# Two GpSimd subtractions of a transformer layer, each cut into pieces of 256 columns

## The chip, the cores and the metric

The kernel runs on one core of a Trainium2 chip. A core has a matrix engine (TensorE, PE in the profile, with its weight loads as PEld), VectorE (DVE), ScalarE (ACT), GpSimd (POOL) and SyncE (SP, which here only issues DMA transfers). Each engine works off its own queue of instructions in order; semaphores make one wait for another. The metric is the time of one execution on the device in microseconds, and a kernel's time is the median of several runs. The profile is one further execution, recorded by the hardware profiler.

## The reference

The function is one layer of a diffusion backbone: 128 context tokens (the prompt) and 512 sample tokens, 640 in all, of width 1024. Cut to what matters here:

```python
def project(h, w_in):                       # 1024 -> 2304 columns
    z = h @ w_in
    qa, ka, va, qb, kb, vb = jnp.split(z, ...)   # 8 neighbourhood heads, 8 window heads on 2 key groups
# for the prompt and for the sample tokens:
h = modulate(rmsnorm(x, g_mix_pre), sh1, sc1)
qa, ka, va, qb, kb, vb = project(h, w_in)        # sample: qb, kb also get a rotary embedding
oa = neighborhood_attn(qa, ka, va, cache_a_k, cache_a_v, rpb_a)
ob = window_attn(qb, kb, vb, cache_b_k, cache_b_v, sink_b)
x = x + gt1 * rmsnorm(concat(rmsnorm(oa, g_a), rmsnorm(ob, g_b)) @ w_out, g_mix_post)
h = modulate(rmsnorm(x, g_ffn_pre), sh2, sc2)
x = x + gt2 * rmsnorm(conv_ffn(h, w_up, conv_w, conv_b, w_down), g_ffn_post)
```

All inputs are fp32, and `sh`, `sc`, `gt` come from a product of the conditioning vectors with `w_mod` (1024 x 6144).

## The kernel before, in words

**Two parts for every operand.** The matrix products run on fp32r operands. Every factor is therefore kept as a high part (`act(hi, src)`, a copy on ScalarE into fp32r) and a low part (`lo = src - hi`), and each product is three matmuls: high by high, high by low, low by high (`mm3`). The low part is a subtraction of two tensors in SBUF, `tt(lo, src, f(hi), ALU.subtract)`, and runs on VectorE, or on GpSimd where `eng=nc.gpsimd` is given. All such subtractions show under line 111 of the profile (the helper `tt`), all ScalarE copies under 108 (`act`), all matmuls of products under 127 (`mm`).

**The stages.** Up to about 60 us the tokens are normalised, transposed and modulated, and the values of the neighbourhood heads are computed. From there to about 330 us the projections and the attention run interleaved. About 280 to 380 us hold the output projection and the second norm, then comes the expansion of the feed-forward part with its convolution (tiles `zx`, `yy`, `wsum`, `ou`, `osb`, to about 650 us), then the contraction (`psd`).

**The streamed weight blocks.** The columns of `w_in` for queries and keys (and the values of the window heads) come in 14 blocks of 1024 x 128, one tile `[128, 8, 128]` each: 1024 columns per partition. The class `Stream` handles them: `load` issues the DMA (line 338, tile `wst`, on SyncE's queue), `split` makes `wh` on ScalarE and `wl` by a subtraction and then issues the next load, and `take` hands a pair to a projection. The pairs have two buffers. The low part of block 0 is made half on VectorE and half on GpSimd, of blocks 1 and 2 on VectorE, of blocks 3 to 13 whole on GpSimd. A projection `tgemm` runs in two chunks of 320 tokens and calls `split` in the middle of the second one; the two projections of one head pair, the keys and values of the window heads and their four query blocks follow each other this way. `tgemm` also carries small products for the modulation (`side_gen`: tiles `wms`, loaded at line 821, results copied to `T` by ScalarE before the next matmuls).

**The attention.** It is a hand-written pipeline of jobs, one per 128 query tokens and head pair. `Pipe.slot` emits the steps of three jobs in turn, and `fill_run` emits steps of the projections between them by estimated costs; so the order on every engine is fixed when the program is built. In a job, TensorE makes the scores (`psS`), VectorE adds the bias or mask and takes the maximum (line 626), ScalarE exponentiates (`P`), the softmax is scaled by VectorE for one head (`soft2`, line 116, tile `P`) and by ScalarE for the other, TensorE transposes (`psT`), and the high and low parts (`ptH`/`ptL`, `pwH`/`pwL`) are made by ScalarE and VectorE. The window heads' queries and keys pass through `rope` on VectorE (tiles `rx`, with a shuffle at line 933) before they are split into `qb` or `kvU`.

**The heads' outputs.** When a head pair's four jobs are done, `o_put` splits its output `o` (512 sample tokens, or 128 prompt tokens) into `oa` or `ob`: the high part on ScalarE, the low part on GpSimd. For the neighbourhood heads the columns are permuted on the way (`jview`, `jsrc`). GpSimd then also adds up squares (`wmsk`, `cs`), clears corners of `ptH`/`ptL`, and copies parts of the bias table (`tab`).

Of the kernel before, what the change touches and what calls it, by code (L numbers as in the profile page):

```python
# [11 lines left out]
ALU = mybir.AluOpType  # L12
# [3 lines left out]
KD = 8  # L16
# [10 lines left out]
def trunk_kernel(  # L27
# [8 lines left out]
    nc = tc.nc  # L36
# [47 lines left out]
    def PB(shape, name, dt=F32):  # L84
        return pp_.tile(shape, dt, tag="p", name=name)
# [15 lines left out]
    def PS(kind, name):  # L101
        return PSB[kind].tile([128, 512], F32, tag=kind, name=name)

    def f(ap):
        return ap.bitcast(F32)

    def act(out, in_, func=ACTF.Copy, **kw):
        return nc.scalar.activation(out=out, in_=in_, func=func, **kw)  # L108

    def tt(out, a, b, op, eng=None):  # L110
        return (eng or nc.vector).tensor_tensor(out=out, in0=a, in1=b, op=op)  # L111
# [10 lines left out]
    def split(hi, lo, src):  # L122
        act(hi, src)
        tt(lo, src, f(hi), ALU.subtract)
# [203 lines left out]
    class Stream:  # L328
# [13 lines left out]
        def split(self):  # L342
            if self.ns < len(self.srcs):
                wh = wr_.tile([128, KD, 128], F32R, tag="wh", name="wh")
                wl = wr_.tile([128, KD, 128], F32R, tag="wl", name="wl")
                w = self.w.pop(self.ns)
                act(wh, w)
                if self.ns:
                    tt(wl, w, f(wh), ALU.subtract, eng=nc.vector if self.ns < 3 else nc.gpsimd)
                else:  # L350
                    for s_, e in ((slice(0, 4), nc.vector), (slice(4, 8), nc.gpsimd)):
                        tt(wl[:, s_], w[:, s_], f(wh[:, s_]), ALU.subtract, eng=e)
                self.s[self.ns] = (wh, wl)
                self.ns += 1
                if self.ns > 1:
                    self.load()
# [163 lines left out]
    def wtile(src, f0):  # L520
        w = WS([128, KD, 128], "wst")
        nc.sync.dma_start(out=w, in_=src[:, f0:f0 + 128].rearrange("(k p) f -> p k f", p=128))
        wh = wr_.tile([128, KD, 128], F32R, tag="wh", name="wh")
        wl = wr_.tile([128, KD, 128], F32R, tag="wl", name="wl")
        split(wh, wl, w)
        return wh, wl
# [42 lines left out]
    def k_ctx(kt, src, step, cnt):  # L569
        def dst(i):  # L570
            v = kt[:, i, :]
            return bass.AP(tensor=v.tensor, offset=v.offset, ap=[list(v.ap[0]), [step, cnt], [1, 128]])
        split(dst(0), dst(1), src.unsqueeze(1).to_broadcast([128, cnt, 128]))
# [10 lines left out]
    def qk_gen(p):  # L584
# [4 lines left out]
        w = stream.take()  # L589
        ps0 = yield from tgemm(w, 0)  # L590
        pend.append(lambda: split(q[:, 0, 0:320], q[:, 1, 0:320], ps0[:, 0:320]))
        ps1 = yield from tgemm(w, 1)
        pend.append(lambda: split(q[:, 0, 320:640], q[:, 1, 320:640], ps1[:, 0:320]))
# [65 lines left out]
    def o_put(o, N, dH, dL, view, t0, n, ss, then=None):  # L659


        act(dH, view(o[:, 0:N]))
        tt(dL, view(o[:, 0:N]), f(dH), ALU.subtract, eng=nc.gpsimd)
        nt = N // 128
        acc = sq_acc["a" if ss is ssA else "b"]
        ac = acc[:, t0 * 128:t0 * 128 + N]
        sqt = PB([128, 512], "sqt")[:, 0:N] if n else ac
        act(jview(sqt) if view is jsrc else sqt, view(o[:, 0:N]), ACTF.Square)
        if n in (1, 2):
            tt(ac, ac, sqt, ALU.add, eng=nc.gpsimd)  # L670
        if n < 2 or (n == 2 and t0):
            return
        if n == 2:
            sqt, t0, nt = acc, 0, 5
        yield 0.22 * nt
        ps_ = PS("o", "psst")
        for t in range(nt):
            nc.tensor.matmul(ps_[:, 2 * t:2 * t + 2], sqt[:, t * 128:t * 128 + 128], ones, start=True, stop=True)
        yield 0.0
        tt(ss[:, t0:t0 + nt], ss[:, t0:t0 + nt], ps_[:, 0:2 * nt:2], ALU.add)  # L680
        if then and n == 2:
            then()
# [5 lines left out]
    jsrc = lambda t: t.rearrange("p (j r c) -> p j r c", j=8, r=8)  # L688

    def natten_jobs(p):  # L690
# [35 lines left out]
        def fin():  # L726
            vc = QK[p][2]
            o = PB([128, 512], "o32")
            for e in range(2):
                ob = PS("o", "psO")  # L730
                h = 2 * p + e
                V = lambda t: Vt[h // 4][:, t, h % 4, :, :].rearrange("p s d -> p (s d)")
                B = lambda a, b, n: tuple(x[:, a:b:n, :] for x in pts[e])
                pv_mm(ob, [
                    (slice(0, 512), vc[:, e, :, :].rearrange("p s d -> p (s d)"), *B(2, 12, 3)),
                    (slice(0, 256), V(2), *B(1, 4, 2)),
                    (slice(128, 384), V(3), *B(4, 7, 2)),
                    (slice(256, 512), V(4), *B(7, 10, 2)),
                    (None, V(1), *B(0, 11, 10)),
                ])  # L740
                yield 0.0 if e else 1.5
                o_sum(o, ob, e, 512)
            yield 0.0
            yield from o_put(o, 512, jview(oa[0][:, p, 128:640]), jview(oa[1][:, p, 128:640]), jsrc, 1, p, ssA)
# [4 lines left out]
    def prompt_job(qkt, ko, V, dst, n, ss, sk, then=None):  # L749
# [43 lines left out]
        def fin():  # L793
            t = t_[0]
            ob = PS("o", "psO")
            for e in range(2):
                cs_ = slice(e * 128, e * 128 + 128)
                pv_mm(ob, [(cs_, V(e), t[:, 0, cs_], t[:, 1, cs_])])
            yield 0.0
            o = PB([128, 512], "o32")  # L800
            for e in range(2):
                o_sum(o, ob[:, e * 128:e * 128 + 128], e, 128)
            yield 0.0
            yield from o_put(o, 128, *dst(), lambda x: x, 0, n, ss, then)
# [221 lines left out]
    def window_jobs(g):  # L1026
# [36 lines left out]
        def fin():  # L1063
            o = PB([128, 512], "o32")
            for kv in range(2):
                ob = PS("o", "psO")
                B = lambda a, b, n: tuple(x[:, a:b:n, :] for x in pts[kv])
                pv_mm(ob, [
                    (slice(0, 512), vbt(5, kv), *B(0, 16, 4)),
                    (slice(0, 256), vbt(1, kv), *B(2, 6, 3)),  # L1070
                    (slice(0, 384), vbt(2, kv), *B(3, 10, 3)),
                    (slice(128, 512), vbt(3, kv), *B(7, 14, 3)),
                    (slice(256, 512), vbt(4, kv), *B(11, 15, 3)),
                ])
                yield 0.0 if kv else 1.7
                o_sum(o, ob, kv, 512)
            yield 0.0
            yield from o_put(o, 512, ob_[0][:, g, 128:640], ob_[1][:, g, 128:640], lambda x: x, 1, g, ssB)
# [930 lines left out]
```

## Time and profile before

| what | value |
|---|---|
| time, median of 3 runs | 835.09 us (829.8 to 836.7) |
| the profiled execution | 831.72 us, span 829.9 us |
| TensorE busy | 797.0 us, 96% of the span |
| VectorE, ScalarE, GpSimd busy | 548.7, 440.1, 294.9 us |
| TensorE's mean granted clock | 0.987 of full |

The span runs from the first to the last instruction; the profiled execution's own time is a little longer. A row of a timeline has the start in us from the span's start, the duration in us, the engine, the line, the operation, `out<-in` by the program's names, and shapes; idle time before it and what ended it stand in brackets. A group of instructions has `busy us, mean ns of one | idle time before`. An instruction's duration includes the time for which it has begun and cannot proceed.

### The profile page before, as it was taken

What the parts mean: (1) busy time and instruction counts of PE and PEld (TensorE: products, weight loads), DVE (VectorE), ACT (ScalarE), POOL (GpSimd) and SP (SyncE); (2) the same over time, 40 slices, a digit from 0 to 9 for tenths busy, and PEclk for the clock granted to TensorE, in tenths of its full rate; (3) what the DMA queues carried; (4) which work ended last, traced back from release to release, by engine and by line L of the source; (5) the groups of instructions that cost most, each with busy time, mean ns of one, the idle gap of its engine ahead of it and who ended that gap; (6) DMA issues with size and microseconds to landing.
All of it is one profiled execution on the core that took longest, in us unless ns stands there. A gap on an engine that the chain in (4) does not pass through costs nothing.

```text
span 829.9 us, 13898 instructions
## 1 busy us (share of the span) xinstructions
PE 797.0 (96%) x5304; PEld 703.5 (85%) x5304; DVE 548.7 (66%) x1023; ACT 440.1 (53%) x876; POOL 294.9 (36%) x345
## 2 busy tenths in 40 slices
PE   6999899999999999999899999999999999999996
PEld 5679778888787777879899999999999978888885
DVE  3555465555889876477888988988988754332115
ACT  5355576645667886467653655655655643331112
POOL 2452444323221211256944656656656000000002
PEclk8999999999999998999999999999999999999999
DMA  9954545536322113656324424424423436424313
GB/s 288 264 167 130 159 110 144 131 107 159 87 60 77 51 52 79 230 181 198 80 67 134 132 85 119 132 84 118 133 84 99 146 117 226 171 102 153 102 51 127
DMA packets 140158, 106.59 MB, mean 128 GB/s; under 512 B 12560, under 2 KB 121388, under 8 KB 140092
## 3 DMA queue, kind: packets, MB, share of 16 engines
q1 hardware_dynamic: 139084, 105.05, 42.5%
q8 instruction: 42, 0.69, 0.3%
q10 hardware_dynamic: 1008, 0.66, 0.3%
q14 instruction: 24, 0.20, 0.1%
HBM read 92.53 MB, written 13.16 MB: 127 GB/s over the span
## 4 chain that ended last, share of the span: by engine, by line
PE 77%; DVE 7%; ACT 5%; DMA 5%; issue 2%; POOL 1%; SPq 0%; DVEq 0%; ACTq 0%; POOLq 0%
PE zx L127 23%; PE psd L127 17%; PE yy L127 9%; PE psg L127 9%; PE psya L127 3%; PE psyb L127 2%; PE psv L127 2%; PE psS L127 2%; PE psO L127 2%; ACT P L108 2%; DMA wms<-in_w_mod_dram 1%; PE psada L371 1%; PE psT L708 1%; DMA vw<-in_w_in_dram 1%; PE psT L1044 1%
## 5 line engine op out<-in xcount | busy, mean ns | idle before, releaser
L127 PE MATMUL psd<-dwh,a 128*128 128x512 f32 x440 | 138.3, 395 | 0.0
L111 POOL TENSOR_TENSOR wsum<-wraw 128x512 f32<-128x512 f32 x36 | 79.0, 2213 | 87.4 <-DVE oc L111 75.6
L127 PEld LDWEIGHTS psd<-dwh,a 128*128 128x128 f32 x440 | 82.9, 188 | 19.7
L127 PE MATMUL zx<-h2H,ou 128*128 128x322 f32 x392 | 94.9, 311 | 0.6 <-DVE yy L111 0.6
L127 PE MATMUL psd<-dwl,a 128*128 128x512 f32 x220 | 87.1, 396 | 0.3 <-DVE dwl L111 0.3
L111 DVE TENSOR_TENSOR dwl<-wd,dwh 128x1024 fp32r<-128x1024 f32 x22 | 26.9, 1225 | 87.9 <-ACT dwh L108 87.9
L127 PE MATMUL psg<-hH,wh 128*128 128x320 f32 x224 | 75.2, 336 | 4.0 <-ACT T L108 3.8
L108 ACT ACTIVATE dwh<-wd 128x1024 fp32r<-128x1024 f32 x22 | 23.3, 1060 | 92.1 <-PE psd L127 85.5
L127 PE MATMUL psg<-hH,wl 128*128 128x320 f32 x224 | 69.9, 312 | 0.0
L127 PE MATMUL psg<-hL,wh 128*128 128x320 f32 x224 | 69.8, 312 | 0.0
L127 PEld LDWEIGHTS zx<-h2H,ou 128*128 128x128 f32 x392 | 68.0, 189 | 0.9 <-DVE yy L111 0.9
L117 POOL TENSOR_SCALAR rdv<-ssdc 128x1 f32<-128x1 f32 x5 | 1.7, 332 | 179.6 <-ACT jk L108 179.6
L127 PE MATMUL zx<-h2L,ou 128*128 128x322 f32 x196 | 60.9, 311 | 0.0
L127 PEld LDWEIGHTS psg<-hH,wh 128*128 128x128 f32 x224 | 42.3, 189 | 12.7 <-ACT T L108 7.4
L127 PEld LDWEIGHTS psd<-dwl,a 128*128 128x128 f32 x220 | 41.3, 188 | 10.4 <-DVE dwl L111 0.7
L108 ACT ACTIVATE cv<-yy,T 128x642 f32<-128x642 f32 x20 | 17.8, 888 | 59.6 <-DVE yy L111 56.0
L111 POOL TENSOR_TENSOR wl<-wst,wh 128x1024 fp32r<-128x1024 f32 (+1 forms) x12 | 27.7, 2310 | 55.9 <-ACT wh L108 39.7
L108 ACT ACTIVATE P<-P,nm 128x320 f32<-128x320 f32 (+3 forms) x64 | 40.3, 630 | 4.9 <-DVE nm L626 4.8
L127 PEld LDWEIGHTS psg<-hL,wh 128*128 128x128 f32 x224 | 42.5, 190 | 0.5
L127 PEld LDWEIGHTS psg<-hH,wl 128*128 128x128 f32 x224 | 42.4, 189 | 0.0
L111 DVE TENSOR_TENSOR ou<-wraw,ou 128x1024 fp32r<-128x1024 f32 x19 | 40.9, 2151 | 0.0
L120 DVE SCALAR_TENSOR_TENSOR cv<-yy,T,cv 128x641 f32<-128x641 f32 x40 | 35.4, 885 | 7.1 <-ACT cv L108 6.2
(360 smaller groups left out, 2189.8 us busy)
## 6 DMA issues: line engine op xcount, KB each, us to landing
wraw<-in_w_up_dram SPq DMA_DIRECT2D x40, 512.0 KB
wms<-in_w_mod_dram SPq DMA_DIRECT2D x30, 512.0 KB
wd<-in_w_down_dram SPq DMA_DIRECT2D x22, 512.0 KB
wm<-in_w_mod_dram SPq DMA_DIRECT2D x16, 512.0 KB
aD<-cv SPq DMA_DIRECT2D x22, 321.0 KB
ar<-aD SPq DMA_DIRECT2D x11, 642.0 KB
wst<-in_w_in_dram SPq DMA_DIRECT2D x10, 512.0 KB
yD<-Y SPq DMA_DIRECT2D x5, 512.0 KB
```

The costliest lines, as they stand in the source:

```text
L108: return nc.scalar.activation(out=out, in_=in_, func=func, **kw)
L111: return (eng or nc.vector).tensor_tensor(out=out, in0=a, in1=b, op=op)
L117: return e.tensor_scalar(out=out, in0=a, scalar1=s1, scalar2=s2, op0=op0, op1=op1)
L120: return nc.vector.scalar_tensor_tensor(out=out, in0=a, scalar=s, in1=b, op0=op0, op1=op1)
L127: return nc.tensor.matmul(out, l, r, start=start, stop=stop, skip_group_check=True, **kw)
L371: nc.tensor.matmul(ps_[32 * g:32 * g + 32, c0:c0 + n], cpad[:, k, :], chunks(k), start=(k < 4), stop=(k >= 4), tile_position=(0, 32 * g), ...
L708: nc.tensor.transpose(pst2[e][:, n * 128:n * 128 + 128], sf[e][0][:, o:o + 128], ident)
L1044: nc.tensor.transpose(pst2[kv][:, n * 128:n * 128 + 128], sf[kv][0][:, c0 * 128:c0 * 128 + 128], ident)
```

## The change

Two subtractions on GpSimd are cut along the columns. The low part of a streamed weight block from block 3 on, one instruction of 1024 columns, becomes four of 256 (two of the eight slices `k` each). The low part of a head pair's output for the 512 sample tokens becomes two instructions of 256 columns; for the neighbourhood heads, where the columns are permuted, the cut is along `j`, so that it is 256 columns there too. The prompt's 128 columns, blocks 0 to 2, and everything else stay.

```diff
@@ Stream.split
-                if self.ns:
-                    tt(wl, w, f(wh), ALU.subtract, eng=nc.vector if self.ns < 3 else nc.gpsimd)
+                if 0 < self.ns < 3:
+                    tt(wl, w, f(wh), ALU.subtract)
+                elif self.ns:
+
+                    for k in range(0, KD, 2):
+                        tt(wl[:, k:k + 2], w[:, k:k + 2], f(wh[:, k:k + 2]), ALU.subtract, eng=nc.gpsimd)
                 else:
@@ o_put
         act(dH, view(o[:, 0:N]))
-        tt(dL, view(o[:, 0:N]), f(dH), ALU.subtract, eng=nc.gpsimd)
+        if N == 512:
+            c3 = (lambda x, i: x[:, 4 * i:4 * i + 4]) if view is jsrc else (lambda x, i: x[:, 256 * i:256 * i + 256])
+            for i in range(2):
+                tt(c3(dL, i), c3(view(o), i), f(c3(dH, i)), ALU.subtract, eng=nc.gpsimd)
+        else:
+            tt(dL, view(o[:, 0:N]), f(dH), ALU.subtract, eng=nc.gpsimd)
         nt = N // 128
```

## The prediction

> **What bounds the kernel now.** I read the page first: how busy TensorE (PE) is, and who stands in the chain of work that ended last.
>
> ```profile
> PE 797.0 (96%) x5304; PEld 703.5 (85%) x5304; DVE 548.7 (66%) x1023; ACT 440.1 (53%) x876; POOL 294.9 (36%) x345
> PE 77%; DVE 7%; ACT 5%; DMA 5%; issue 2%; POOL 1%; SPq 0%; DVEq 0%; ACTq 0%; POOLq 0%
> ```
>
> TensorE is busy for 797.0 of 829.9 us, and GpSimd (POOL) has almost no share of the chain. So making GpSimd quicker or slower by itself is worth nothing; what can pay is time in which GpSimd stops another engine that TensorE then waits for. VectorE's 7% of the chain is where to look. The groups of GpSimd by shape give the instructions that the change touches:
>
> ```profile
> L111 POOL TENSOR_TENSOR wl<-wst,wh 128x1024 fp32r<-128x1024 f32 x11 | 26.4, 2403 | 55.9 <-ACT wh L108 39.7 <-PE pstb L960 11.6 <-DVE rc L636 3.2
> L111 POOL TENSOR_TENSOR wl<-wst,wh 128x512 fp32r<-128x512 f32 x1 | 1.3, 1288 | 0.0
> L111 POOL TENSOR_TENSOR ob<-o,ob 128x512 fp32r<-128x512 f32 x4 | 5.4, 1340 | 34.2 <-ACT ob L108 34.2
> L111 POOL TENSOR_TENSOR oa<-o,oa 128x512 fp32r<-128x512 f32 x4 | 5.1, 1279 | 8.0 <-ACT oa L108 7.9
> ```
>
> Eleven weight subtractions of about 2.4 us and eight head subtractions of about 1.3 us. I then took the timeline of VectorE (DVE) around each of the nineteen and looked for VectorE instructions longer than others of their shape. For eight of the eleven weight blocks and all eight head outputs there is none above half a microsecond too long. Three weight blocks have one each. Undisturbed, the two shapes concerned take 0.42 and 0.36 us:
>
> ```profile
> 198.66 0.42 DVE L116 TENSOR_SCALAR P<-P,rc 128x384 f32<-128x384 f32 x1
> 183.99 0.36 DVE L111 TENSOR_TENSOR rx<-rx,cs 128x192 f32<-128x192 f32 x1
> ```
>
> Here are the three, in rows picked from the timelines of the engines (start, duration, engine, and in brackets the idle time and what ended it; rows between them are left out):
>
> ```profile
> 184.01 2.57 POOL L111 TENSOR_TENSOR wl<-wst,wh 128x1024 fp32r<-128x1024 f32 x1 [11.58 <-PE pstb L960]
> 184.26 2.54 DVE L116 TENSOR_SCALAR P<-P,rc 128x384 f32<-128x384 f32 x1
> 186.73 0.35 DVE L111 TENSOR_TENSOR rx<-rx 128x192 f32<-128x192 f32 x1
> 187.11 0.36 ACT L108 ACTIVATE kvU<-rx 128x192 fp32r<-128x192 f32 x1 [1.80 <-DVE rx L111]
> 187.69 0.42 PE L127 MATMUL psg<-hH,wh 128*128 128x320 f32 x1 [1.13 <-ACT T L108]
> ```
>
> ```profile
> 211.54 2.38 POOL L111 TENSOR_TENSOR wl<-wst,wh 128x1024 fp32r<-128x1024 f32 x1 [9.68 <-ACT wh L108]
> 211.56 2.57 DVE L111 TENSOR_TENSOR rx<-rx,cs 128x192 f32<-128x192 f32 x1
> 214.25 0.34 DVE L111 TENSOR_TENSOR rx<-rx 128x192 f32<-128x192 f32 x1
> 215.02 0.36 DVE L111 TENSOR_TENSOR qb<-rx,qb 128x192 fp32r<-128x192 f32 x1
> 215.04 0.84 PE L127 MATMUL psS<-kvU,qb 64*128 64x384 f32 x6 [1.81 <-ACT qb L108]
> ```
>
> ```profile
> 233.26 2.37 POOL L111 TENSOR_TENSOR wl<-wst,wh 128x1024 fp32r<-128x1024 f32 x1 [3.24 <-DVE rc L636]
> 233.29 2.56 DVE L116 TENSOR_SCALAR P<-P,rc 128x384 f32<-128x384 f32 x1
> 236.34 0.17 DVE L116 TENSOR_SCALAR nm<-mx 128x2 f32<-128x2 f32 x1
> 236.41 0.69 DVE L111 TENSOR_TENSOR pwL<-psT,pwH 128x512 fp32r<-128x512 f32 x1
> 237.16 0.68 PE L1044 MATMUL psT<-ident,P 128*128 128x128 f32 x3 [1.73 <-DVE pwL L111]
> ```
>
> Each time a VectorE instruction on SBUF operands lasts until about 0.2 us after the GpSimd instruction's end (186.80 against 186.58, 214.13 against 213.92, 235.85 against 235.63): it stands still for some 2.1 us. TensorE's idle time behind the three is 1.13 + 1.81 + 1.73 = 4.67 us, and all three stand in the chain. That is the most the change can win directly.
>
> **Does VectorE get in between two pieces?** In the expansion stage GpSimd runs two 512-column instructions back to back beside VectorE:
>
> ```profile
> 520.59 1.22 DVE L111 TENSOR_TENSOR osb<-wsum,osb 128x1024 fp32r<-128x1024 f32 x1
> 520.75 2.22 POOL L111 TENSOR_TENSOR wsum<-wraw 128x512 f32<-128x512 f32 x1 [4.48 <-DVE oc L111]
> 521.80 2.25 DVE L111 TENSOR_TENSOR ou<-wraw,ou 128x1024 fp32r<-128x1024 f32 x1
> 522.92 2.28 POOL L111 TENSOR_TENSOR wsum<-wraw 128x512 f32<-128x512 f32 x1
> ```
>
> Read the ends: `osb` ends at 521.81; `wsum`, begun earlier, ends 1.16 us after that; `ou` ends 1.08 us after `wsum` (524.05 against 522.97); the second `wsum`, already queued, ends 1.15 us after `ou` (525.20). They take strict turns. So a waiting VectorE instruction should wait for the piece in progress only, and a queued piece then goes before the next VectorE instruction that needs the same access.
>
> **The change, term by term.** *Length of the pieces.* From 1288 ns for 512 columns and 2403 ns for 1024: 2.18 ns a column and 173 ns fixed, so 256 columns come to 731 ns, four to 2.92 us. That is 0.52 us more on GpSimd for each weight block (5.7 us over eleven), and for a head output 2 x 0.73 against about 1.31 us, 0.15 us more (1.2 us over eight). A few of these nanoseconds overlap from one instruction to the next, so this is the upper end.
>
> *Where that length lies.* Nobody on TensorE waits for the low parts: these are its four largest waits between 78 and 330 us, and GpSimd isn't in the rest of that list either (waited in all, times, longest):
>
> ```profile
> PE psg L127 <- ACT T L108: 3.8, 6, 1.1
> PE psg L371 <- DMA wms<-in_w_mod_dram: 2.6, 3, 1.2
> PE psT L1044 <- DVE pwL L111: 2.2, 3, 1.7
> PE psS L127 <- ACT qb L108: 1.8, 1, 1.8
> ```
>
> A weight block is split a whole block ahead of its use (two buffers), so its cover is one block's share of the work; the consecutive blocks of 211.54 and 233.26 stand 21.7 us apart. The queue of SyncE is nearer: the next block's load waits for the last piece.
>
> ```profile
> SPq L338 <- POOL wl L111: 7.8, 4, 2.4
> 129.87 0.37 SPq L338 DMA_DIRECT2D wst<-in_w_in_dram  x1
> 130.33 2.46 SPq L247 DMA_DIRECT2D traw<-scr  x4
> 132.90 6.52 SPq L821 DMA_DIRECT2D wms<-in_w_mod_dram  x2
> ```
>
> At 129.87 the load leaves, and the loads of the bias table and of the modulation weights stand directly behind it; TensorE waits for the latter three times in the list above. A piece more of 0.52 us there costs TensorE between 0 and 0.5 us, where it has no slack; I take 0.2, once, since in the list that wait is the exception. The head outputs' extra 0.15 us is hidden where their follower waits for ScalarE anyway:
>
> ```profile
> 305.52 1.29 POOL L111 TENSOR_TENSOR cs<-cs,sqt 128x512 f32<-128x512 f32 x1 [1.02 <-ACT sqt L108]
> ```
>
> No VectorE instruction is held long by a head output, so that half of the change is worth 0. Without the cover it costs at most 1.2 us.
>
> *First stall.* GpSimd itself started about 0.17 us late (2.57 against 2.40), so the first piece ends near 184.01 + 0.17 + 0.73 = 184.91, `P` 0.22 later at 185.13. The addition `rx` then waits for the second piece, to 185.86, and ends near 186.1 instead of 187.08. ScalarE's two steps and TensorE move up by 1.0 of the 1.13 us: TensorE ran out at 186.56.
>
> *Second stall.* First piece to 212.27, `rx` to 212.48, second piece to 213.21, the addition to 213.45 instead of 214.59: 1.14 us. The low part of `qb` must wait for the third piece and is then late for the last matmuls of the scores by about 0.2 us. 0.9 us.
>
> *Third stall.* First piece to 233.99, `P` to 234.21 instead of 235.85; `nm` meets the second piece and loses 0.3; `pwL` ends near 235.76 instead of 237.10. 1.35 us.
>
> Together 1.0 + 0.9 + 1.35 = 3.25 us. Bounds: 4.67 if every piece boundary falls well, and below nothing if no turns are taken (next part).
>
> *The granted clock.* Behind the third gap TensorE ran slowly:
>
> ```profile
> 214.00:216.00 2.00, 0.96 (x8) 0.68 (x9) 1.97 (x9) 0.53 (x2) 0.00 (x0) 1.00 0.80 221
> 236.00:238.00 2.00, 0.84 (x5) 0.85 (x6) 1.93 (x9) 1.85 (x8) 0.24 (x3) 0.86 0.60 168
> 238.00:240.00 2.00, 2.00 (x9) 1.90 (x8) 1.50 (x8) 0.91 (x5) 0.19 (x1) 0.50 1.06 334
> 240.00:242.00 2.00, 2.00 (x12) 1.96 (x11) 1.73 (x7) 0.77 (x4) 0.00 (x0) 0.79 0.09 22
> ```
>
> The clock column is the third from the right. The loss is 2 x (0.14 + 0.50 + 0.21) = 1.7 us, right after a gap of 1.73 us; yet the gap of 1.81 us before 215.04 left the clock at 1.00. So a gap of this size can bring the slow stretch and need not. With the gap cut to about 0.4 us I expect it to go; bounds 0 and 1.7, and I take 1.2 for the chance that another gap brings one. The Trainium skill speaks against this term: "TensorE: Matmul & The Clock Gate", "Why this matters for your kernels", wants idle gaps of over about 3 us for a drop. By that rule a gap of 1.73 us causes nothing and the term is 0. The trace has its drop behind a shorter gap, so it does not bear the rule out here, but the untouched clock after 1.81 us leaves it a chance (second rival).
>
> **The sum**, against the profiled execution of 831.72 us (span 829.9): -3.25 - 1.2 + 0.2 = -4.25 us, so 827.5 us. That execution was 0.4% below the median of the three runs, 835.09; the same difference from the median gives 830.8 us, a ratio of 0.995.
>
> **Rivals.** *Pieces do not give way.* If a queued piece went before the waiting VectorE instruction, the three stalls would last 2.92 us instead of 2.4: 3 x 0.52 = 1.6 us slower, 836.7. It decides as soon as GpSimd's next piece is requested before VectorE is served. The turns at 520 to 525 us speak against it; for it, that those were pairs, not fours, and longer. Chance 8%. This is the case on the slower side.
>
> *Turns are taken, the clock stays as it is*: the slow stretch does not hang on this gap, or another gap brings one. Then -3.25 + 0.2, so 832.0 us; the untouched clock behind 1.81 us speaks for it. Chance 27%. The page of the Trainium skill named above would have it this way.
>
> *The gain is taken back by the next wait.* TensorE comes sooner to ScalarE's copies of `T` (six waits, 3.8 us) or to a VectorE that is busy for 1.93, 1.50 and 1.73 of 2 us in the last three rows of the clock's view, and all but 1 us goes: 834. Chance 17%. For it: VectorE still has to sit out the other pieces. Against: the stage after it is TensorE's, so what arrives early stays early.
>
> *More than expected*: a second slow stretch of the clock goes as well, and the time passes -1%: 826. Chance 6%. *Nothing done*, the pieces joined again: no reason for it, 1%; slower by over 1% would take 8 us, more than all lengthening together (6.9), so 2% for what I don't see.
>
> **The numbers.** My forecast has 39%: 830.8 us, with its own range 828 to 833. The range must also hold the rivals (832.0, 834, 836.7) and the runs' own spread, 829.8 to 836.7 for one kernel; I give 825.5 to 836.9. About 1% is what a measurement of this kernel can tell from no change; the forecast and nearly all rivals lie within it. Faster by over 1% has the 6% and the lower edge of the forecast, 14%; slower by over 1%, 3%; within, 83%.
>
> **What would show it.** In the changed trace: 44 weight pieces of about 0.73 us and 16 head pieces; no VectorE instruction held for 2 us by one of them, but more that are held for up to 0.7; the waits of TensorE on `T`, `qb` and `pwL` shorter by about 1, 0.9 and 1.3 us; the clock at 1.00 near 238 us; GpSimd about 7 us busier; the later stages as long as before, only sooner. I am wrong if a VectorE instruction still lasts 2.5 us beside the pieces, or if TensorE's gaps shrink and the end does not move.

## The result and the profile after

The changed kernel takes 827.42 us (median of 15 runs, 825.2 to 831.51); the kernel before, run beside it, 833.0 us (15 runs, 828.21 to 836.7). The ratio of the two sets' means is 0.9944, interval 0.9926 to 0.9962 (the medians alone give 0.9933): about half a per cent faster, which the 1% named in the prediction counts as no change. The profiled execution took 826.45 us, its span is 824.6 us and its mean granted clock 0.988 (before 831.72, 829.9 and 0.987).

The page of the changed kernel, engines and the chain's shares:

```profile
PE 797.2 (97%) x5304; PEld 702.4 (85%) x5304; DVE 547.7 (66%) x1023; ACT 440.9 (53%) x876; POOL 301.9 (37%) x386
PE 76%; DVE 6%; ACT 5%; DMA 4%; issue 2%; POOL 1%; SPq 0%; DVEq 0%; ACTq 0%; POOLq 0%
```

TensorE has the same work. VectorE's share of the chain fell from 7 to 6%, and GpSimd is busy for 7.0 us more (301.9 against 294.9), in 41 more instructions (33 for the blocks, 8 for the heads). The groups that the change touched, by shape, with busy time and mean ns:

```profile
L111 POOL TENSOR_TENSOR wl<-wst,wh 128x256 fp32r<-128x256 f32 x44 | 32.2, 760 | 54.0 <-ACT wh L108 39.4 <-PE pstb L969 11.1 <-DVE rc L640 3.2
L111 POOL TENSOR_TENSOR ob<-o,ob 128x256 fp32r<-128x256 f32 x8 | 5.9, 761 | 34.4 <-ACT ob L108 34.4
L111 POOL TENSOR_TENSOR oa<-o,oa 128x256 fp32r<-128x256 f32 x8 | 5.7, 734 | 6.1 <-ACT oa L108 6.0
```

Now the three places at which VectorE had stood still, in rows picked from the timelines of the changed kernel's engines. First:

```profile
183.91 3.37 POOL L111 TENSOR_TENSOR wl<-wst,wh 128x256 fp32r<-128x256 f32 x4 [11.08 <-PE pstb L969]
184.16 0.90 DVE L116 TENSOR_SCALAR P<-P,rc 128x384 f32<-128x384 f32 x1
184.97 0.90 DVE L111 TENSOR_TENSOR rx<-rx 128x192 f32<-128x192 f32 x1
186.49 0.42 PE L127 MATMUL psg<-hH,wh 128*128 128x320 f32 x1
```

`P` took 2.54 us and now takes 0.90; the addition `rx`, 0.35 before, now sits out the second piece and takes 0.90 too. The matmul at 186.49 has no idle time in front of it any more (1.13 us before). Second:

```profile
210.38 3.17 POOL L111 TENSOR_TENSOR wl<-wst,wh 128x256 fp32r<-128x256 f32 x4 [9.28 <-ACT wh L108]
210.38 0.93 DVE L111 TENSOR_TENSOR rx<-rx,cs 128x192 f32<-128x192 f32 x1
211.44 0.70 DVE L111 TENSOR_TENSOR rx<-rx 128x192 f32<-128x192 f32 x1
212.59 0.85 PE L127 MATMUL psS<-kvU,qb 64*128 64x384 f32 x6 [0.54 <-ACT qb L108]
212.87 0.95 DVE L116 TENSOR_SCALAR P<-P,rc 128x128 f32<-128x128 f32 x2
```

2.57 us became 0.93, and TensorE's gap 0.54 instead of 1.81 us. Third:

```profile
231.28 2.93 POOL L111 TENSOR_TENSOR wl<-wst,wh 128x256 fp32r<-128x256 f32 x4 [3.24 <-DVE rc L640]
231.32 0.92 DVE L116 TENSOR_SCALAR P<-P,rc 128x384 f32<-128x384 f32 x1
232.72 0.17 DVE L116 TENSOR_SCALAR nm<-mx 128x2 f32<-128x2 f32 x1
233.54 0.55 PE L1053 MATMUL psT<-ident,P 128*128 128x128 f32 x3
233.59 0.64 DVE L111 TENSOR_TENSOR es<-nm,sink 128x2 f32<-128x2 f32 x1
234.95 0.55 PE L1053 MATMUL psT<-ident,P 128*128 128x128 f32 x3 [0.28 <-DVE pwL L111]
```

The transposition that stood behind a gap of 1.73 us starts at 233.54 with none. A small one is new one step later: the last piece holds `es` for 0.64 us (0.16 before), and the next transposition waits 0.28 us. TensorE's waits between 183 and 240 us, the whole list (in all, times, longest):

```profile
PE psS L127 <- ACT qb L108: 0.5, 1, 0.5
PE psT L1053 <- DVE pwL L111: 0.3, 1, 0.3
PE psT L717 <- DVE vb L111: 0.2, 1, 0.2
```

Of 4.67 us, 0.82 are left (0.54 + 0.28).

**How far ahead TensorE comes.** Gaps that close can open elsewhere. So I compared the starts of the same matmuls in two traces. At the matmul `psg` at 180.41 us of the kernel before, ahead of all three places, the changed kernel is 0.12 us ahead. Behind the first place it is 1.20 ahead (187.69 against 186.49), behind the second 2.45 (215.04 against 212.59), then 1.97, and behind the third 3.62 (237.16 against 233.54). It won 3.62 - 0.12 = 3.50 us there. Where 0.48 were lost between, the rows of the weight loads and of the next transposition show. Of before:

```profile
217.18 0.29 PEld L127 LDWEIGHTS psS<-kvU,qb 64*128 64x128 f32 x2 [0.20 <-issue]
218.26 0.44 PE L784 MATMUL psT<-ident,P 128*128 128x128 f32 x2
```

And after:

```profile
214.87 0.30 PEld L127 LDWEIGHTS psS<-kvU,qb 64*128 64x128 f32 x2 [0.33 <-DVE nm L630]
215.41 0.29 PEld L127 LDWEIGHTS psS<-kvU,qb 64*128 64x128 f32 x3 [0.24 <-DVE nm L630]
216.29 0.44 PE L793 MATMUL psT<-ident,P 128*128 128x128 f32 x2
```

The loads for the next scores now wait twice for VectorE's maximum `nm`, inside a group of matmuls, so that the list of TensorE's waits doesn't show it: VectorE hasn't become earlier by as much as TensorE has, because it still sits out the later pieces (`P` at 212.87 beside the last of them). The lead shrinks to 218.26 - 216.29 = 1.97.

### The profile page after: what moved, and what is told of

Its sections match the earlier page's. It is cut to its first block, busy times and chain, and to the rows that moved or that the text cites. A ratio compares the mean times of both kernels' runs of the same rounds, so it can differ in the third digit from the quotient of the medians.

```text
span 824.6 us, 13946 instructions
## 1 busy us (share of the span) xinstructions
PE 797.2 (97%) x5304; PEld 702.4 (85%) x5304; DVE 547.7 (66%) x1023; ACT 440.9 (53%) x876; POOL 301.9 (37%) x386
## 4 chain that ended last, share of the span: by engine, by line
PE 76%; DVE 6%; ACT 5%; DMA 4%; issue 2%; POOL 1%; SPq 0%; DVEq 0%; ACTq 0%; POOLq 0%
PE zx L127 23%; PE psd L127 17%; PE yy L127 9%; PE psg L127 8%; PE psya L127 3%; PE psyb L127 2%; PE psS L127 2%; PE psO L127 2%; DMA wms<-in_w_mod_dram 2%; PE psv L127 2%; ACT P L108 2%; PE psT L1053 1%; PE psg L375 1%; PE psT L717 1%; PE psada L375 1%
## 5 line engine op out<-in xcount | busy, mean ns | idle before, releaser
L111 POOL TENSOR_TENSOR wl<-wst,wh 128x256 fp32r<-128x256 f32 (+1 forms) x45 | 33.5, 772 | 54.0 <-ACT wh L108 39.4
```

## The experiments

Times of one kernel spread over up to 12 us, and most of that goes with the granted clock. I therefore also fitted the times of all 252 runs (99 of before, 27 of the changed kernel, 12 each of most others) with one offset for each kernel and a common slope against the mean granted clock: 0.001 of clock is worth 0.66 us (plus or minus 0.04), and what is left over scatters by 1.1 us. "At equal clock" below is the offset against before from that fit, with its 95% interval. For the changed kernel it is -3.9 (plus or minus 0.6) in the first 15 runs. It leaves out whatever a kernel wins or loses through its clock; in plain means the changed kernel is 4.7 us ahead of before in the first set and 5.2 us in the second. Each experiment ran beside the kernel before on its own chip, on three chips in all; the ratios are those on record, which differ a little from the quotients of the medians or the means. "Ahead" is the count made above: the lead of TensorE at three matmuls (behind the first and second place and behind the third, 187.69, 215.04 and 237.16 of before), less the lead at 180.41.

| kernel | ratio, interval | at equal clock, us | ahead, us |
|---|---|---|---|
| the change | 0.9944 (0.9926 to 0.9962) | -3.9 ± 0.6 | 1.08, 2.33, 3.50 |
| the change again | 0.9947 (0.9924 to 0.9969) | -3.7 ± 0.7 | 1.20, 2.49, 3.66 |
| blocks only | 0.9938 (0.9911 to 0.9964) | -4.0 ± 0.7 | 1.20, 2.50, 3.66 |
| heads only | 1.0016 (0.9988 to 1.0045) | +0.8 ± 0.7 | 0.00, -0.04, -0.04 |
| two pieces | 0.9987 (0.9963 to 1.001) | -1.1 ± 0.7 | 0.00, 0.19, -0.44 (clock) |
| three blocks | 0.9963 (0.9939 to 0.9987) | -2.9 ± 0.7 | 1.10, 2.34, 3.50 |
| three blocks again | 0.9948 (0.9924 to 0.9973) | -2.8 ± 0.7 | 1.09, 2.34, 3.51 |
| the other eight | 0.9994 (0.997 to 1.0019) | 0.0 ± 0.7 | 0.05, 0.01, 0.02 |
| eight pieces | 0.995 (0.9925 to 0.9976) | -4.1 ± 0.7 | 1.29, 3.11, 4.36 |
| no low part of three blocks | 0.9899 (0.9856 to 0.9942) | -5.3 ± 1.0 | 1.21, 3.06, 5.14 |
| three blocks on VectorE | 0.9929 (0.9902 to 0.9955) | -3.3 ± 0.7 | 1.19, other order, other order |
| values in pieces too | 0.9944 (0.9918 to 0.9971) | -3.6 ± 0.7 | 1.20, 2.44, 3.61 |
| more pieces | 0.9945 (0.9919 to 0.9972) | -3.0 ± 0.7 | not counted |

**One half at a time.** The weight blocks alone, as an edit of before:

```diff
-                    tt(wl, w, f(wh), ALU.subtract, eng=nc.vector if self.ns < 3 else nc.gpsimd)
+                    if self.ns >= 3:
+                        for k in range(0, KD, 2):
+                            tt(wl[:, k:k + 2], w[:, k:k + 2], f(wh[:, k:k + 2]), ALU.subtract, eng=nc.gpsimd)
+                    else:
+                        tt(wl, w, f(wh), ALU.subtract, eng=nc.vector if self.ns < 3 else nc.gpsimd)
```

> Only the weight blocks in four pieces, the heads' outputs whole as before. Turns theory (VectorE stands behind the whole GpSimd instruction, and gets in between two pieces): the whole gain of the change, ratio 0.994 to 0.996 against the kernel before, with no VectorE instruction held for 2 us by a weight block. Rival (the heads' outputs bring a share): at least 0.15% of the 0.56% is missing, ratio 0.9960 or above.

And the heads' outputs alone, the weight blocks whole:

```diff
-        tt(dL, view(o[:, 0:N]), f(dH), ALU.subtract, eng=nc.gpsimd)
+        if N == 512:
+            c3 = (lambda x, i: x[:, 4 * i:4 * i + 4]) if view is jsrc else (lambda x, i: x[:, 256 * i:256 * i + 256])
+            for i in range(2):
+                tt(c3(dL, i), c3(view(o), i), f(c3(dH, i)), ALU.subtract, eng=nc.gpsimd)
+        else:
+            tt(dL, view(o[:, 0:N]), f(dH), ALU.subtract, eng=nc.gpsimd)
```

> Only the heads' outputs in two pieces, the weight blocks whole as before. Turns theory: no VectorE instruction was held long by a head output, so ratio 1.000 with an uncertainty of 0.002, and the three stalls of about 2.1 us still there. Rival (the heads' outputs bring a share): ratio 0.998 or below.

Measured: 827.25 against 831.83 us for the blocks, 832.97 against 831.83 for the heads. The blocks carry the whole gain, the heads none. At equal clock the heads alone even come out 0.8 us slower, at the edge of what the runs can tell, but the blocks with the heads are no slower than the blocks without (-3.9 and -3.7 against -4.0). I have no cause for the 0.8 us, and it stays open.

**Two pieces instead of four**, where turns and no turns differ most (the lines that differ from the edit for the blocks alone):

```diff
+                        for k in range(0, KD, 4):
+                            tt(wl[:, k:k + 4], w[:, k:k + 4], f(wh[:, k:k + 4]), ALU.subtract, eng=nc.gpsimd)
```

> The weight blocks in two pieces of 512 columns, the heads' outputs whole. Turns theory: at the first two stalls the first held instruction is freed after about 1.3 us, but the second piece then goes ahead of the next VectorE instruction that needs the same access (the addition of rx), which ends within 0.2 us of where it ended before; at the third stall 0.2 to 0.5 us are won. So almost nothing: ratio 0.9990 to 1.0005, and two VectorE instructions of about 1.5 us at each of the first two stalls. Rival (what counts is the length of the piece that VectorE meets): half of the gain, ratio about 0.997. Rival (the clock alone): somewhere between, with the waits of TensorE unchanged.

Rows from the timelines of the kernel with two pieces (the first place, then the matmuls behind the second and third):

```profile
184.89 2.83 POOL L111 TENSOR_TENSOR wl<-wst,wh 128x512 fp32r<-128x512 f32 x2 [11.54 <-PE pstb L964]
185.14 1.44 DVE L116 TENSOR_SCALAR P<-P,rc 128x384 f32<-128x384 f32 x1
186.51 1.43 DVE L111 TENSOR_TENSOR rx<-rx 128x192 f32<-128x192 f32 x1
188.56 0.41 PE L127 MATMUL psg<-hH,wh 128*128 128x320 f32 x1 [1.12 <-ACT T L108]
215.72 0.53 PE L127 MATMUL psS<-kvU,qb 64*128 64x384 f32 x2 [1.60 <-ACT qb L108]
238.47 0.55 PE L1048 MATMUL psT<-ident,P 128*128 128x128 f32 x3 [1.13 <-DVE pwL L111]
```

This is the turn-taking at its plainest. `P` gets through behind the first piece and ends at 186.58 (185.14 + 1.44); the second piece, already queued, goes next, and `rx` gets through only behind it. One long hold has become two of half the length, and TensorE's first gap is as long as it was, 1.12 against 1.13 us. All three gaps shrink from 4.67 to 3.85 us, and at equal clock the kernel is 1.1 us faster (plus or minus 0.7): less than the half of the gain that the rival names, though the ratio's interval, 0.9963 to 1.001, would still hold it; the rows decide it. (Its lead at 237.16 is negative because a stretch of 4 us behind the second place, 216 to 220, ran at a clock of 0.58, which cost 4 x 0.42 = 1.7 us; with that added back it is 1.2 us.)

**Which blocks.** The three that stop TensorE alone, and later the other eight alone (of the second edit only the line that differs):

```diff
+                    if self.ns in (10, 12, 13):
+                        for k in range(0, KD, 2):
+                            tt(wl[:, k:k + 2], w[:, k:k + 2], f(wh[:, k:k + 2]), ALU.subtract, eng=nc.gpsimd)
```

> Only the blocks 10, 12 and 13 in four pieces, the ones that held VectorE for 2 us; the other eight whole, the heads' outputs whole. Turns theory: the whole gain, ratio 0.994 to 0.996. Rival (many small holds at the other blocks add up): a third or more of the gain is missing, ratio 0.9962 or above.

> The kernel with only the blocks 10, 12 and 13 in four pieces once more, beside the changed kernel on the same chip. Turns theory: the same as the changed kernel within 0.8 us at equal clock. Rival (the other eight blocks or the heads bring a share): 1 us or more behind it.

```diff
+                    if self.ns >= 3 and self.ns not in (10, 12, 13):
```

> The kernel before, with the blocks 3 to 9 and 11 in four pieces and the blocks 10, 12 and 13 whole; heads whole. At equal clock three blocks alone won 2.8 us and all eleven 4.0. Turns theory: the other eight hold VectorE by no more than a quarter of a microsecond each and TensorE waits for none of it, so 0 with an uncertainty of 0.8 us, and the three gaps of 1.1, 1.8 and 1.7 us stay. Rival (many small holds add up): about 1.1 us less than before at equal clock.

> The changed kernel once more, on the same chip as the three others. Turns theory: 3.2 to 4.7 us less than before at equal clock (gaps of 4.67 us fall to about 0.8), ratio 0.994 to 0.996. Clock theory (a share of the gain is a slow stretch that goes): its mean granted clock lies above that of the kernel before by 0.001 or more.

The other eight alone do nothing, 832.54 against 833.15 us and 0.0 us at equal clock, and their trace still has the long holds; a row of its timeline:

```profile
213.74 2.57 DVE L111 TENSOR_TENSOR rx<-rx,cs 128x192 f32<-128x192 f32 x1
```

The three alone bring TensorE just as far ahead as all eleven do (3.50 and 3.51 us against 3.50 and 3.66). Yet twice their time at equal clock came out at -2.8 to -2.9, where all eleven have -3.7 to -4.0. The two halves, -2.8 and 0.0, fall about a microsecond short of the whole. The second set of the three is 0.84 us behind the changed kernel beside it at equal clock, where I had expected 0.8 at most; yet in the times as they are it is ahead, 826.54 against 827.78 us. It is near what such a fit can tell, and where that microsecond would lie I couldn't find: the waits between 183 and 245 us are the same. Open.

**How much more there is.** Eight pieces of 128 columns, and, as the ceiling, no low part at all for the three blocks (the matmuls read the high part in its place; this leaves out three of the weights' low parts, and has 6 runs). The first is an edit of the changed kernel, the second of before:

```diff
+                    for k in range(0, KD):
+                        tt(wl[:, k:k + 1], w[:, k:k + 1], f(wh[:, k:k + 1]), ALU.subtract, eng=nc.gpsimd)
```

> The changed kernel with eight pieces of 128 columns for a weight block (about 0.46 us each, 3.7 us together). Turns theory: VectorE is held for at most about 0.5 us by each piece; the waits of TensorE that the change left at the second and third stall (0.54 and 0.28 us) fall below 0.3 and 0.2, the first has nothing left. 0.3 to 0.8 us less than the changed kernel, ratio 0.993 to 0.995 against the kernel before. Rival (each piece more is a turn lost): VectorE is held just as long in sum, and the time is that of the changed kernel or up to 1 us above it.

```diff
+                    if self.ns not in (10, 12, 13):
+                        tt(wl, w, f(wh), ALU.subtract, eng=nc.vector if self.ns < 3 else nc.gpsimd)
...
+                self.s[self.ns] = (wh, wh if self.ns in (10, 12, 13) else wl)
```

> The kernel before, but the low parts of blocks 10, 12 and 13 are not made at all (the high part is used in their place in the matmuls, whose number and shapes stay): GpSimd then holds nothing at the three places, so this is the most that any cutting can win there. Turns theory: TensorE's idle time of 4.67 us behind the three goes but for a few tenths, 4.2 to 4.9 us at equal clock, ratio 0.994 to 0.995, 0.3 to 1 us better than the changed kernel. Rival (the gain came from elsewhere, such as the other eight blocks or the clock): ratio 0.997 or above.

Eight pieces, from the timeline:

```profile
188.16 3.94 POOL L111 TENSOR_TENSOR wl<-wst,wh 128x128 fp32r<-128x128 f32 x8 [10.36 <-PE pstb L969]
188.41 0.62 DVE L116 TENSOR_SCALAR P<-P,rc 128x384 f32<-128x384 f32 x1
```

`P` is down to 0.62 us, no wait for `qb` is left, and the lead is 4.36 us instead of 3.5. In the times that 0.8 us is hardly there (-4.1 against -3.9, each plus or minus 0.6 to 0.7). The ceiling has none of the three gaps, a lead of 5.14 and -5.3 us (plus or minus 1.0), where I had expected 4.2 to 4.9. Its ratio of 0.9899 is lower than that because its six runs also had a higher mean clock, 0.990 against 0.986 of before on that chip. So by the lead the change takes some 3.5 of the 5.1 us that these three subtractions cost the kernel.

**Off GpSimd altogether**: the three blocks' low parts on VectorE, everything else as before.

```diff
+                    tt(wl, w, f(wh), ALU.subtract, eng=nc.vector if self.ns < 3 or self.ns in (10, 12, 13) else nc.gpsimd)
```

> The kernel before, with the low parts of blocks 10, 12 and 13 made whole on VectorE (1.23 us each) instead of GpSimd. Turns theory (the price was 2.1 us of VectorE standing still each time): VectorE now loses 1.23 us instead of 2.1 to 2.2 at each place, so about 0.9 us less for each, 2 to 2.7 us in all at equal clock, ratio about 0.997, less than the change wins. Rival (VectorE's own load does not matter there, only GpSimd's hold): as good as the change, ratio 0.994 to 0.995. Rival (VectorE must also wait for ScalarE's high part in its order): no gain.

The three in its timeline, and TensorE in front of the scores at the second place:

```profile
188.07 1.21 DVE L111 TENSOR_TENSOR wl<-wst,wh 128x1024 fp32r<-128x1024 f32 x1
211.36 1.23 DVE L111 TENSOR_TENSOR wl<-wst,wh 128x1024 fp32r<-128x1024 f32 x1
231.67 1.23 DVE L111 TENSOR_TENSOR wl<-wst,wh 128x1024 fp32r<-128x1024 f32 x1
212.93 0.39 PE L127 MATMUL psO<-ptH,k 128*128 128x512 f32 x1
214.45 0.80 PE L127 MATMUL psS<-kvU,qb 64*128 64x384 f32 x6
```

VectorE does in 1.2 us what GpSimd does in 2.4, and at its own place in VectorE's queue: at 188.07 it comes after the steps that TensorE waits for, where GpSimd's came in front of them. TensorE has none of the three gaps between 183 and 245 us, and the time, 826.39 against 832.48 us, is as good as the change's. So my forecast of 2 to 2.7 us and a ratio of about 0.997 came out low (3.3 us, plus or minus 0.7, and 0.9929), and the first rival is what happened: moving three subtractions did what cutting eleven did. Why as much as this isn't shown. At the second and third place the subtraction still stands in front of the held steps, but the order of TensorE's matmuls came out differently in this kernel: at the second place some `psO` and more `psg` now run in front of the scores, and they fill time in which TensorE had stood idle.

**More of the same.** GpSimd's other long instructions have VectorE instructions held beside them too. The values' low parts in pieces of 256 columns, added to the change; and then also the sums for the expansion (`fg`) in pieces of 256:

```diff
-            tt(wl[:, j], vw[st][:, j], f(wh[:, j]), ALU.subtract, eng=nc.gpsimd)
+            for i in range(j.start, j.stop):
+                for c0 in (0, 256):
+                    s_ = slice(c0, c0 + 256)
+                    tt(wl[:, i, s_], vw[st][:, i, s_], f(wh[:, i, s_]), ALU.subtract, eng=nc.gpsimd)
```

> The changed kernel with the low parts of the value weights in pieces of 256 columns too, and without the pieces of the sums for the expansion that were given back. Turns theory: up to 1.2 us less than the changed kernel, where TensorE waits for hL near 45 us, and nothing where the weights' transfer arrives at another moment, so 0 to 1.2 us, 0.5 likely. Rival (the values' weights arrive too late for it to matter): the same time as the changed kernel.

```diff
-        if t < 3:
-            tt(g_, f(h2H[1][:, :, c_]), f(h2L[1][:, :, c_]), ALU.add, eng=nc.gpsimd)
-        tt(g_, g_, f_, ALU.subtract, eng=nc.gpsimd)
+        for i in (slice(0, 2), slice(2, 4)):
+            if t < 3:
+                tt(g_[:, i], f(h2H[1][:, i, c_]), f(h2L[1][:, i, c_]), ALU.add, eng=nc.gpsimd)
+        for i in (slice(0, 2), slice(2, 4)):
+            tt(g_[:, i], g_[:, i], f_[:, i], ALU.subtract, eng=nc.gpsimd)
```

> The changed kernel, and two more groups of GpSimd subtractions and additions in pieces of 256 columns: the low parts of the value weights (1024 or 512 columns, near 19 to 54 us) and the sums for the expansion (512 columns, near 382 to 396 us). In the changed kernel's trace two scalings of VectorE last 2.89 us at 42.5 us beside such an instruction (0.80 elsewhere) and TensorE then waits 1.4 us for the low part behind them; at 386 to 391 us four VectorE instructions are longer than their shape by 0.9 us and all stand in the chain. Turns theory: 0.8 to 1.2 us less at the first place, 0.8 to 1.8 at the second, so 1.6 to 3 us less than the changed kernel, ratio 0.990 to 0.993 against the kernel before. Rival (a later wait takes it back: the values' weights wait for their transfer, and the expansion for its weights): ratio 0.994 as the changed kernel.

Neither beats the change: 828.47 against 833.15 us, and 828.37 against 832.48. With the values in pieces the lead behind the three places is as before, and nothing is won beyond it (-3.6 at equal clock). For the two together the 1.6 to 3 us forecast didn't come. What happens with `fg` is worth reading. TensorE's waits between 370 and 470 us, first of the changed kernel, then of the one with more pieces:

```profile
PE zx L127 <- ACT raw L108: 2.1, 1, 2.1
```

```profile
PE yy L127 <- DVE pwl L111: 2.0, 1, 2.0
PE zx L127 <- ACT raw L108: 0.8, 1, 0.8
```

The first wait falls by 1.3 us, as it should, and 40 us later one of 2.0 us is new. GpSimd has hardly any slack here: its sums run one behind the other, from 382.10 to 396.73 us in the changed kernel (14.63 us) and from 384.50 to 400.07 with more pieces (15.57 us, single pieces of 0.74 us lasting up to 1.82). ScalarE's gate `tg` waits for the last of them and VectorE's chain for the gate. The last sum so ends 0.94 us later, counted from the first; VectorE ends `pwl` about 1 us later, counted the same way, while TensorE comes 1.27 us sooner. Less the 0.25 us by which `pwl` had been early, that is the new wait. By the starts of the same matmuls TensorE is 1.27 us better off behind the first wait and 0.85 us worse off behind the second.

## Why the prediction was right, and where it was not

The forecast was a ratio of 0.995; measured is 0.9944. 827.42 us lies 3.4 us below the forecast 830.8 and just below its own range of 828 to 833, within the full one; 2.1 of the 3.4 us are that the median of before came down from 835.09 (3 runs) to 833.0 (15 runs). Against the before that ran beside it, the change won 4.7 us in the means (832.7 to 828.0), where the sum had 4.25. That is near, but not every term was right, and for one of them the forecast was a guess.

*What bounds the kernel* held: the gain comes from the three holds of VectorE. The other eight blocks are worth 0.0 (plus or minus 0.7); the heads win nothing: 0.8 us (plus or minus 0.7) slower alone, no difference beside the blocks.

*Length of the pieces*: 731 ns forecast, 760 and 734 to 761 measured, 7.0 us more on GpSimd against 6.9. For the blocks the added length costs nothing that the runs can tell; for the heads the 0.8 us above is open.

*Turns*: confirmed. No VectorE instruction is held for 2.5 us, those directly behind it are held as well, and the kernel with two pieces shows the turn as such. With that the slower rival (pieces that don't give way, 836.7 us) is out.

*The stalls*, 1.0 + 0.9 + 1.35 = 3.25 us forecast. The lead says 1.08, then 1.25 less 0.48, then 1.65: 3.50. The first was right. For the second I had a net 0.9 and it is 1.25 - 0.48 = 0.77, with another reason for the loss than the one I gave: not the low part of `qb`, but the maximum `nm` for the next scores. So the rival "taken back by the next wait" happened, for 0.5 us of the gain and not for most of it. The third was under-sized by 0.3: `nm`, which I let meet the second piece, runs free (0.17 us), and the step that is held instead, `es`, costs 0.28 one transposition later.

*SyncE's queue*, +0.2: not seen. TensorE's wait for `wms` between 78 and 330 us is 1.7 us in the changed kernel's trace instead of 2.6. The other eight blocks alone, where that lengthening would show by itself, have 0.0 (plus or minus 0.7).

*The granted clock*, -1.2 us: this was the term with the least under it, one slow stretch in one trace, at 236 to 242 us behind the gap there. The other runs speak for it that such gaps cost clock, though not each of them. The kernel with the heads alone has the same gap and no slow stretch (a row of its timeline, then one of its table by stretches, where the clock is third from the right):

```profile
241.13 0.55 PE L1049 MATMUL psT<-ident,P 128*128 128x128 f32 x3 [1.74 <-DVE pwL L111]
```

```profile
242.00:244.00 2.00, 2.00 (x14) 1.65 (x13) 2.00 (x12) 1.31 (x6) 0.18 (x1) 1.00 1.04 325
```

The one with the other eight blocks has the same gap and a slow stretch behind it, in the same two views:

```profile
239.33 0.55 PE L1048 MATMUL psT<-ident,P 128*128 128x128 f32 x3 [1.74 <-DVE pwL L111]
```

```profile
240.00:242.00 2.00, 2.00 (x11) 1.84 (x10) 1.70 (x9) 1.37 (x7) 0.32 (x1) 0.54 1.07 351
```

And the one with two pieces has its slow stretch behind the second place, whose gap of 1.60 us it kept:

```profile
216.00:220.00 4.00, 4.00 (x21) 2.96 (x19) 3.37 (x12) 2.01 (x6) 1.15 (x7) 0.58 0.64 150
```

So of the four traces in which TensorE still has gaps of over 1 us at the three places, three have a slow stretch behind one of them, each costing 1.7 us. The ten traces without these gaps have none between 183 and 300 us. These are single executions, and few. The row of the changed kernel, which is also the sign that I had named (a clock of 1.00 near 238 us):

```profile
213.00:245.00 32.00, 31.56 (x239) 26.15 (x236) 27.76 (x91) 24.16 (x64) 9.50 (x26) 1.00 0.28 76
```

It has slow stretches elsewhere. Its stretches of 4 us from 302 on, and the only line on TensorE's waits from 294 to 310 us:

```profile
302.00:306.00 4.00, 3.48 (x21) 2.34 (x19) 3.18 (x8) 3.75 (x9) 1.65 (x5) 1.00 0.01 2
306.00:310.00 4.00, 4.00 (x18) 2.78 (x17) 3.25 (x10) 2.35 (x6) 0.00 (x0) 0.61 0.00 0
310.00:314.00 4.00, 4.00 (x14) 3.11 (x14) 1.29 (x4) 1.68 (x3) 0.00 (x0) 0.53 0.16 57
```

```profile
PE psT L1053 <- DVE pwL L111: 0.5, 2, 0.2
```

There the clock falls to 0.61 and 0.53 behind two waits of 0.2 us, so a slow stretch doesn't need a gap of over 1 us. But at the three places it came only with one.

The mean clock of the runs points the same way. The changed kernel's second set has 0.9878 against 0.9856 for before on the same chip, 0.0022 more (plus or minus 0.0021); I had named 0.001 as the sign of a share of the clock. For the seven experiments that cut the three blocks into four pieces or more, taken together against the runs on the same chips that keep the gaps, it is 0.0015 (plus or minus 0.0009). At 0.66 us for each 0.001 that makes 1.0 us (plus or minus 0.6). The times at equal clock can't show this share, since they take it out. So the forecast of 1.2 lies within what the runs show, and the rival "turns are taken, the clock stays" is not what they favour. It was lucky all the same: a choice between 0 and 1.7 from one trace. Why one gap brings a slow stretch and the next doesn't stays open.

The page of the Trainium skill that I had set against the term ("TensorE: Matmul & The Clock Gate", "Why this matters for your kernels") asks only that TensorE have no idle gaps of over about 3 us. The traces don't bear that out here: slow stretches came behind gaps of 1.60, 1.73 and 1.74 us, and others behind waits of 0.2 us.

Together: the sum had 3.25 us for the stalls, 1.2 for the clock and 0.2 of cost for the queue. The runs show 3.5 us for the stalls by the lead (3.9 by the times at equal clock), about 1 us for the clock, and nothing that can be told from 0 for the queue. The term that was mis-sized most is the third stall, by 0.3 us; the one that no run shows is the queue's 0.2.

## What to carry to other kernels

When GpSimd and VectorE hold each other up on SBUF operands, what counts is not how long GpSimd's work is but how long one instruction of it is, and how many VectorE instructions lie between the hold and the matmul that waits: with a queued piece going ahead of each of them, two pieces won 1.1 us, four 3.9 at equal clock. Cut, or move to VectorE where it has the time, only the instructions whose holds end in a TensorE gap; where GpSimd itself is on the path, as with `fg`, cutting makes it later. And follow the same matmuls through both traces: the lead at each shows what a stall was worth net, to a tenth of a microsecond as long as no slow stretch lies between, where a list of waits hides part of what is lost again. Comparing at equal clock narrows the scatter, but it hides what a change wins through the clock itself; look at the mean clocks too.

## What the runs showed of the hardware

The strict turns reach down to the smallest pieces: with 128 columns (474 ns on average) the held `P` takes 0.62 us. A VectorE instruction of only two columns can be held as well (`es`, 128x2: 0.64 us instead of 0.16).

The granted clock goes down for short stretches. In the fourteen traces each of them, from 20 us on until TensorE's last matmul, costs it 1.7 us, or two or three times that (306 to 314 us of the changed kernel, above: 4 x 0.39 + 4 x 0.47 = 3.4). They lie at a handful of places, such as 23 to 28, 153 to 162 and 305 to 321 us, and which of these an execution has changes from run to run. Most of the scatter between runs of one kernel goes with the clock: 0.66 us for each 0.001 of its mean. Comparing at equal clock left a scatter of 1.1 us, so that differences of 0.7 us could be told in 12 runs.
